# One decoder layer with 32 experts: big and small expert positions as two interleaved tracks of one-slot items, with a ninth weight slot

## The chip, the core and the metric

The kernel runs on one core of one Trainium2 chip. The metric is device time in microseconds (us) of one execution; the median of several runs is quoted with its lowest and highest. Engines: PE (TensorE, matmuls), DVE (VectorE), ACT (ScalarE), POOL (GpSimd) and SP (SyncE, which here issues DMAs).

## The reference

A residual stream of 512 tokens by 1024 channels passes one decoder layer in float32: RMSNorm, one input projection, a causal pooling mixer beside multi-head latent attention, an output projection and the residual; then the mixture of experts, which is what the change is about, and a final RMSNorm. Each token goes to 4 of 32 experts:

```python
logits = (ht @ w_router + b_router).astype(jnp.float32)
top_vals, top_idx = lax.top_k(logits, TOP_K)          # TOP_K = 4 of N_EXPERTS = 32
gates = jax.nn.softmax(top_vals, axis=-1)
...
gu = xblk @ w_gate_up[e] + b_gate_up[e]               # 1024 x 2048
gate = jnp.minimum(gu[:, :D_EXPERT], SWIGLU_LIMIT)
up = jnp.clip(gu[:, D_EXPERT:], -SWIGLU_LIMIT, SWIGLU_LIMIT)
act = gate * jax.nn.sigmoid(SWIGLU_ALPHA * gate) * (up + 1)
return act @ w_down[e] + b_down[e]                    # 1024 x 1024
```

So each expert needs 8 MiB of gate-and-up weights and 4 MiB of down weights, and all 32 are read: 384 MiB, about 403 MB.

## The kernel before

**The start.** Up to about 220 us the kernel does the attention half, the router and the choice of experts. Weights of expert position 0 are loaded beside it. Positions 0 to 31 are experts sorted by how many tokens chose them; which expert stands at a position is known on the chip only (`eid`, read into SP's registers).

**Big and small.** `KINDS` names each position B or S: 13 big ones (0, 4, 6, 8 and so on to 26) for up to 128 tokens, 19 small ones for up to 64. A loop after the main one takes what overflows.

- A *big* position has each weight tile split into a high and a low fp32r part: ACT casts (`mhi`, L875), DVE or POOL subtracts (`mlo`, L876), a helper `split` on 128x1024 halves with four buffers for each part. PE then does three matmuls for each product (`mm3`, L95 to L97, for gate and up; L979 for down). DVE or POOL is chosen by a fixed rule: POOL has 9 of a position's 24 halves, five in gate-and-up, four in down.
- A *small* position multiplies plain fp32 weights out of the slot in which they landed, 64 tokens wide, two such matmuls side by side in the array (L919 gate and up, L1001 down).

**The stages of a position.** `gather` transposes its tokens' rows (fetched by an indirect DMA on POOL's queue) into `xgh`/`xgl` or `xgs`; `gate_up` makes the gate and up sums in PSUM banks; `act`/`swiglu` is the nonlinearity on DVE and ACT; `turn` transposes the result (`ath`/`atl`, `ats`); `down` is the second product; `combine` scatters it to the tokens with matmuls into an `m` bank, and DVE adds that to `y` (L1059).

**The order.** The list `steps` says in which order whole `gate_up` and `down` stages stand: from position 6 on `gu` of a big, `gu` of a small, `dn` of the big, `dn` of the small. Other work (`rest`, `turned`, `arriving`, `gathering`) is put between the stage's items by generators, one step for each item. Before a big `gate_up`, `split_ahead` splits its first three items while the small `down` before it runs; a `down` has nothing split ahead. A scheduler then places the instructions of each engine in the order in which its own model finds them ready, so an engine's final order is not the program's line by line. Each engine runs its final order strictly in turn.

**Slots and loads.** Weights land in a ring of eight 1 MiB slots (one k of gate-and-up, or two k of down). SP issues the loads in ring order, and each waits until its slot has been read. PSUM has six `gu` banks, which all gate, up and down sums share, and two `m` banks.

Of the kernel before, what the change touches and what calls it, by code (L numbers as in the profile page):

```python
# [11 lines left out]
F32 = mybir.dt.float32  # L12
# [11 lines left out]
P = 128  # L24
# [17 lines left out]
assert len(KINDS) == 32 and KINDS[0] == "B" and "BB" not in KINDS and KINDS.endswith("SS") and NBIG % 2 == 1  # L42
# [3 lines left out]
NPRE = 3  # L46
# [54 lines left out]
def block_kernel(ctx: ExitStack, tc: tile.TileContext, xT, x, pos, vecs, w_in, w_pool, w_qb, w_kvb, w_out,  # L101
# [640 lines left out]
    def bank(tag):  # L742
        return pools["pm"].tile([P, T], F32, tag=tag, bufs={"gu": 6, "m": 2}[tag], name=tag)


    nslot = [0]

    def slot():
        i = nslot[0] % (NRING + 4 + NRINGB)
        nslot[0] += 1  # L750
        return (ring if i < NRING else qk if i < NRING + 4 else ringb).tile([P, 2 * D], F32, tag="slot", name="slot")
# [3 lines left out]
    def load_gate_up(r, w):  # L755
        for k in range(KD):
            wslots[r, "gu", k] = slot()
            dma(wslots[r, "gu", k], w[k * P:(k + 1) * P, :])

    def load_down(r, w, halves=False):  # L760

        n = 4 if halves else 2
        for c in range(2 if halves else 1):
            for k in range(KD // n):
                v = slot().rearrange("p (a d) -> p a d", a=n)
                cs = slice(c * T, (c + 1) * T) if halves else slice(0, D)
                dma(v, w[n * k * P:n * (k + 1) * P, cs].rearrange("(a p) d -> p a d", p=P))
                for a in range(n):
                    wslots[r, "dn", n * k + a, c] = v[:, a, :]
# [3 lines left out]
    def load_expert(r, e):  # L773

        gu, wdown[r] = (w[e] if isinstance(e, int) else w[bass.ds(e, 1)].rearrange("a k d -> (a k) d")
                        for w in (w_gate_up, w_down))
        load_gate_up(r, gu)

    load_expert(0, 0)
# [7 lines left out]
    def big(r):  # L787
        return r == "o" or KINDS[r] == "B"

# [18 lines left out]
    rows, idxs = {}, {}  # L808

    def fetch(r):  # L810
# [8 lines left out]
        rows[r] = hbp.tile([P, D], F32, tag="hb", name="xr")  # L819
# [39 lines left out]
    def slot_info(r, ax=None):  # L859
# [6 lines left out]
        sl = mo.tile([P, 7], F32, tag="sl", bufs=6, name="sl")  # L866
# [12 lines left out]
    presplit = {}  # L879

    def split_ahead(r):

        for k in range(NPRE):
            for hf in range(2):
                presplit[r, k, hf] = split(wslots[r, "gu", k][:, hf * D:(hf + 1) * D], G if hf else V)

    def gate_up(r, *beside):
        banks = [bank("gu") for _ in range(4 if big(r) else 2)]

        def biases():  # L890
            for c in range(4):
                bs = bias[:, c * T:(c + 1) * T]
                if big(r):
                    PE.matmul(banks[c], lhsT=m4b[0:96, r:r + 1].to_broadcast([96, P]), rhs=bs, start=r > 0, stop=r == 0)
                else:
                    q = 64 * (c % 2)
                    PE.matmul(banks[c // 2][q:q + 64, :], lhsT=m4b[0:96, r:r + 1].to_broadcast([96, 64]), rhs=bs,
                              start=True, stop=False)


        first = r == 0 or r == "o"
        if not first:
            biases()
        for k in range(KD):
            w = wslots.pop((r, "gu", k))
            if big(r):

                todo = [(hf, c) for hf in range(2) for c in range(2)] if k < KD - 1 else [
                    (hf, c) for c in range(2) for hf in range(2)]
                parts = [presplit.pop((r, k, hf), None) or  # L910
                         split(w[:, hf * D:(hf + 1) * D], G if (2 * k + hf) % 4 == 1 else V) for hf in range(2)]
                for hf, c in todo:
                    cs = slice(c * T, (c + 1) * T)
                    mm3(nc, banks[2 * hf + c], xg[r][0][:, k, :], xg[r][1][:, k, :], parts[hf][0][:, cs],
                        parts[hf][1][:, cs], first and k == 0, r != 0 and k == KD - 1)
            else:
                for c in range(4):
                    q = 64 * (c % 2)
                    PE.matmul(banks[c // 2][q:q + 64, :], lhsT=xg[r][:, k, :], rhs=w[:, c * T:(c + 1) * T],  # L919
                              start=False, stop=(k == KD - 1))  # L920
            for v in beside:
                next(v, None)
        if r == 0:
            biases()
        return banks
# [16 lines left out]
    def act(r, banks):  # L942
        return [swiglu(banks[c], banks[2 + c]) for c in range(2)] if big(r) else [swiglu(*banks)]

    def turn(r, us_):
# [5 lines left out]
        else:  # L951
            at = mo.tile([P, 2, 4, 64], F32, tag="ats", bufs=1, name="ats")
# [15 lines left out]
    def down(r, *beside):  # L968
        if big(r):
            hi, lo = actT.pop(r)  # L970
            banks = [bank("gu") for _ in range(2)]
            for k in range(KD):
                for v in beside:
                    next(v, None)
                wh, wl = split(wslots[r, "dn", k, 0], G if k % 2 == 0 else V)

                for n, (a, b) in enumerate(((hi, wh), (hi, wl), (lo, wh))):
                    for c in range(2):
                        PE.matmul(banks[c], lhsT=a[:, k, :], rhs=b[:, c * T:(c + 1) * T], start=(k == 0 and n == 0),  # L979
                                  stop=(k == KD - 1 and n == 2))  # L980
# [3 lines left out]
            for c in range(2):  # L984
                S.activation(yh[:, c], banks[c], AF.Copy, scale=ga_)  # L985
                V.scalar_tensor_tensor(yl[:, c], banks[c], ga_, yh[:, c].bitcast(F32), op0=ALU.mult, op1=ALU.subtract)  # L986
# [4 lines left out]
        else:  # L991
            at = actT.pop(r)
            db = bank("gu")
            par = KINDS[:r].count("S") % 2
            for k in range(KD):
                for v in beside:
                    next(v, None)
                w = wslots[r, "dn", k, 0]
                for q in range(2):
                    c = q ^ par  # L1000
                    PE.matmul(db[64 * q:64 * q + 64, :], lhsT=at[:, k, :], rhs=w[:, c * T:(c + 1) * T],  # L1001
                              start=(k == 0), stop=(k == KD - 1))
            if par == 0:
# [13 lines left out]
    def down_last(r, gf):  # L1017
# [7 lines left out]
        for c in range(2):  # L1025
            cs = slice(c * T, (c + 1) * T)

            pb = [bank("gu") for _ in range(NT)]
# [3 lines left out]
            db = bank("gu")  # L1032
            for k in range(KD):

                q = 64 * (k % 2)
                PE.matmul(db[q:q + 64, :], lhsT=at[:, k, :], rhs=wslots[r, "dn", k, c], start=(k < 2),  # L1036
                          stop=(k >= KD - 2))
# [9 lines left out]
    def combine(keys, with_bias=False, after=None):  # L1047


        parts = [(c, sc, [v[:, c] for v in yb[key]]) for key in keys for c, sc in enumerate(scat.pop(key))]  # L1050
# [233 lines left out]
    for r in range(6, E, 2):  # L1284
        steps += [("gu", r), ("gu", r + 1), ("dn", r), ("dn", r + 1)]
# [193 lines left out]
```

## Time and profile before

| | |
|---|---|
| median of 3 runs | 1412.95 us (1412.23 to 1414.8) |
| the profiled execution | 1414.44 us, of which the span from first to last instruction is 1412.7 us |
| PE busy in the span | 1271.1 us (90%), 5657 matmuls |
| DVE, ACT, POOL busy | 923.4 us (65%), 568.6 us (40%), 447.2 us (32%) |
| read from HBM | 430.24 MB, 308 GB/s over the span |

A busy PE is not a PE at its peak: matmuls overlap in the trace, so two that are 0.39 us long start 0.23 us apart. What a stretch is worth is read from how many matmuls it holds, from PE's idle time and from the granted clock (1.00 is 2.4 GHz, 0.50 is 1.2 GHz).

### The profile page before, as it was taken

To read this page: it belongs to the slowest core of one execution; us is meant where nothing else is said; L and a number is where in the kernel's file an instruction comes from. 1 tells how busy PE (TensorE), PEld (TensorE's weight loads), DVE (VectorE), ACT (ScalarE), POOL (GpSimd) and SP (SyncE) were. 2 spreads that over 40 slices of the span, in tenths; PEclk is the share of its full clock that TensorE was granted. 3 is DMA by queue.
4 is the path that set the end of the run, shared out by engine and by line. 5 is a ranking of instruction groups with operands and counts; after the bars stand their busy time and mean duration, and the time that the engine had idled before them with its cause. 6 is when DMAs were issued, how large, how long until landed. Compare 5 with 4: busy or idle time off the path is not lost.

```text
span 1412.7 us, 16684 instructions
## 1 busy us (share of the span) xinstructions
PE 1271.1 (90%) x5657; PEld 735.4 (52%) x5657; DVE 923.4 (65%) x1482; ACT 568.6 (40%) x819; POOL 447.2 (32%) x298
## 2 busy tenths in 40 slices
PE   7989977998989898998989898998899899999984
PEld 6756665534546464645546464645455454643322
DVE  6897689345757587676667586677766676853313
ACT  5477545113334353533334443534343535420112
POOL 1545363102143343323143443333241524330001
PEclk9999989899999999999999999999999999999997
DMA  7213336699999988897979899999979899899992
GB/s 296 75 58 118 138 131 224 241 413 424 411 399 351 336 333 337 328 347 291 346 302 353 330 354 338 340 336 348 359 293 365 328 329 360 340 333 382 424 421 107
DMA packets 87060, 435.71 MB, mean 308 GB/s; under 512 B 9209, under 2 KB 9337, under 8 KB 54202
## 3 DMA queue, kind: packets, MB, share of 16 engines
q1 hardware_dynamic: 82964, 420.57, 78.4%
q0 software_dynamic: 3808, 13.63, 2.5%
q8 instruction: 46, 0.75, 0.2%
q10 hardware_dynamic: 198, 0.39, 0.1%
q14 instruction: 44, 0.36, 0.1%
HBM read 430.24 MB, written 4.33 MB: 308 GB/s over the span
## 4 chain that ended last, share of the span: by engine, by line
PE 35%; issue 14%; DVE 5%; DMA 5%; POOL 4%; ACT 1%; POOLq 0%; DVEq 0%; ACTq 0%
PE gu L919 7%; PE gu L979 5%; PE gu L1001 5%; DMA slot<-in_w_down_dram 4%; PE gu L96 4%; PE gu L97 4%; PE gu L95 4%; POOL mlo L876 4%; DVE mlo L876 3%; PE m L1058 3%; DMA slot<-in_w_gate_up_dram 1%; ACT mhi L875 1%; PE m L849 1%; POOL xr L820 1%; PE gu L1036 1%
## 5 line engine op out<-in xcount | busy, mean ns | idle before, releaser
L876 POOL TENSOR_TENSOR mlo<-slot,mhi 128x1024 fp32r<-128x1024 f32 x116 | 316.8, 2737 | 586.8 <-ACT mhi L875 584.9
L876 DVE TENSOR_TENSOR mlo<-slot,mhi 128x1024 fp32r<-128x1024 f32 x196 | 350.8, 1817 | 40.9 <-ACT mhi L875 39.8
L875 ACT CAST mhi<-slot 128x1024 fp32r<-128x1024 f32 x312 | 317.6, 1049 | 148.8 <-PE gu L97 95.1
L919 PE MATMUL gu<-slot,xgs 128*64 128x512 f32 x1216 | 284.2, 600 | 2.2 <-DMA slot<-in_w_gate_up_dram 2.2
L96 PE MATMUL gu<-mlo,xgh 128*128 128x512 f32 x416 | 168.6, 405 | 19.7 <-DVE mlo L876 10.9
L97 PE MATMUL gu<-mhi,xgl 128*128 128x512 f32 x416 | 164.5, 395 | 0.0
L919 PEld LDWEIGHTS gu<-slot,xgs 128*64 128x64 f32 x1216 | 79.3, 136 | 154.9 <-issue 147.2
L1001 PE MATMUL gu<-slot,ats 128*64 128x512 f32 x576 | 139.9, 617 | 2.8 <-DMA slot<-in_w_down_dram 2.1
L1059 DVE TENSOR_TENSOR y<-y,m 128x512 f32<-128x512 f32 x120 | 81.0, 683 | 78.4 <-PE m L1058 77.2
L95 PE MATMUL gu<-mhi,xgh 128*128 128x512 f32 x416 | 125.2, 399 | 0.0
L936 ACT ACTIVATE as<-ag 128x512 f32<-128x512 f32 x45 | 28.4, 631 | 235.0 <-DVE ag L935 235.0
L96 PEld LDWEIGHTS gu<-mlo,xgh 128*128 128x128 f32 x416 | 79.2, 190 | 52.4 <-DVE mlo L876 16.9
L979 PE MATMUL gu<-mlo,ath 128*128 128x512 f32 x208 | 78.7, 463 | 24.4 <-POOL mlo L876 16.4
L979 PE MATMUL gu<-mhi,ath 128*128 128x512 f32 x208 | 73.3, 436 | 21.1 <-ACT mhi L875 20.4
L95 PEld LDWEIGHTS gu<-mhi,xgh 128*128 128x128 f32 x416 | 77.6, 190 | 20.4 <-issue 4.1
L97 PEld LDWEIGHTS gu<-mhi,xgl 128*128 128x128 f32 x416 | 79.4, 191 | 15.8
L820 POOL DMA_INDIRECT xr<-hrow,idx x22 | 33.8, 1536 | 143.7 <-DVE idx L818 80.5
L1001 PEld LDWEIGHTS gu<-slot,ats 128*64 128x64 f32 x576 | 37.4, 139 | 75.6 <-issue 67.0
L979 PE MATMUL gu<-mhi,atl 128*128 128x512 f32 x208 | 72.5, 433 | 0.0
L935 DVE TENSOR_SCALAR ag<-gu 128x512 f32<-128x512 f32 x45 | 31.0, 689 | 63.3 <-PE gu L919 60.5
L1014 DVE SCALAR_TENSOR_TENSOR ysl<-gu,sl,ysh 64x512 fp32r<-64x512 f32 x36 | 26.9, 748 | 67.1 <-ACT ysh L1012 66.6
L986 DVE SCALAR_TENSOR_TENSOR ybl<-gu,sl,ybh 128x512 fp32r<-128x512 f32 x26 | 18.3, 746 | 78.4 <-ACT ybh L985 78.4
(390 smaller groups left out, 1744.5 us busy)
## 6 DMA issues: line engine op xcount, KB each, us to landing
slot<-in_w_gate_up_dram SPq DMA_DIRECT2D x256, 1024.0 KB, 6.9
slot<-in_w_down_dram SPq DMA_DIRECT2D x128, 1024.0 KB, 7.5
wraw<-in_w_in_dram SPq DMA_DIRECT2D x16, 256.0 KB, 5.0
wraw<-in_w_out_dram SPq DMA_DIRECT2D x16, 256.0 KB, 2.5
xtraw<-in_xT_dram SPq DMA_DIRECT2D x8, 256.0 KB, 6.2
y<-in_x_dram SPq DMA_DIRECT2D x4, 512.0 KB, 6.8
hrow<-part POOLq DMA_DIRECT2D x8, 256.0 KB, 2.9
out_dram<-o SPq DMA_DIRECT2D x4, 512.0 KB, 3.6
```

The lines of the kernel that those rows point to most:

```text
L95: nc.tensor.matmul(out, lhsT=shi, rhs=mhi, start=first, stop=False)
L96: nc.tensor.matmul(out, lhsT=shi, rhs=mlo, start=False, stop=False)
L97: nc.tensor.matmul(out, lhsT=slo, rhs=mhi, start=False, stop=last)
L820: G.indirect_dma_start(out=rows[r], out_offset=None, in_=hrow, in_offset=bass.IndirectOffsetOnAxis(ap=idx[:, 0:1], axis=0), bounds_check=T ...
L875: S.copy(hi, src)
L876: eng.tensor_tensor(lo, src, hi.bitcast(F32), op=ALU.subtract)
L919: PE.matmul(banks[c // 2][q:q + 64, :], lhsT=xg[r][:, k, :], rhs=w[:, c * T:(c + 1) * T], start=False, stop=(k == KD - 1))
L935: V.tensor_scalar(g, gb, 7.0, None, op0=ALU.min)
L979: PE.matmul(banks[c], lhsT=a[:, k, :], rhs=b[:, c * T:(c + 1) * T], start=(k == 0 and n == 0), stop=(k == KD - 1 and n == 2))
L1001: PE.matmul(db[64 * q:64 * q + 64, :], lhsT=at[:, k, :], rhs=w[:, c * T:(c + 1) * T], start=(k == 0), stop=(k == KD - 1))
L1058: PE.matmul(pb, lhsT=a, rhs=b, start=(i == 0), stop=(i == len(todo) - 1))
L1059: V.tensor_tensor(y[:, t, cs], y[:, t, cs], pb, op=ALU.add)
```

## The change

Whole stages no longer stand one behind the other. Each position is cut into twelve *items* of one slot each, eight of `gate_up` and four of `down`. Two tracks are made: `tx` with the items of all big positions (and of the last small one), `ty` with the items of the other 18 small positions. A small search (`interleave`) merges them into one static `plan`: it pays for each change of track (`TURN`), for a `down` that starts fewer than `GAPX` = 5 small or `GAPY` = 2 big items after its own `gate_up` (`SHORT`), and for running ahead or behind of an even mix. The plan that results has 127 blocks, 64 of the big track and 63 of the small track, mostly two to five items long. Other edits go with it:

- Splits are made item by item (`split_item`), the next two items of the big track ahead of the one that PE multiplies, `down` items too. POOL has one half in four, DVE three; so of a position's 24 halves POOL has 6 and DVE 18.
- The six shared PSUM banks become four for the big track (`x`) and two for the small track (`y`).
- Loads are listed in the order in which slots are read: a small block's loads stand behind those of the big block after it, since that one is split ahead.
- A ninth slot is taken from one of the two `hb` buffers; fetched rows share the other.
- Down weights of the last position are loaded in four pieces as plan items.

```diff
+GAPX, GAPY, GAPEND = 5, 2, 3
+TURN, SHORT = 0.2, 3.0
...
-        return pools["pm"].tile([P, T], F32, tag=tag, bufs={"gu": 6, "m": 2}[tag], name=tag)
+        return pools["pm"].tile([P, T], F32, tag=tag, bufs={"x": 4, "y": 2, "m": 2}[tag], name=tag)
...
+    nring = NRING + 4 + NRINGB + 1
+    pair = []
...
+        if i == nring - 1:
+            if not pair:
+
+                pair.append(hbp.tile([P, 2, D], F32, tag="hb", name="xr"))
+            return hbp.tile([P, 2 * D], F32, tag="hb", name="slot")
...
-        rows[r] = hbp.tile([P, D], F32, tag="hb", name="xr")
+        rows[r] = pair[0][:, nfetch[0] % 2, :]
...
+    def split_item(r, what, k):
+
+        w = wslots.pop((r, what, k))
+        out_ = []
+        for hf in range(2):
+            out_.append(split(w[:, hf * D:(hf + 1) * D], G if nsplit[0] % 4 == 1 else V))
+            nsplit[0] += 1
+        presplit[r, what, k] = out_
...
-    steps = [("gu", 0), ("dn", 0), ("gu", 1), ("gu", 2), ("dn", 1), ("gu", 3), ("dn", 2), ("gu", 4), ("dn", 3),
-             ("gu", 5), ("dn", 4), ("dn", 5)]
-    for r in range(6, E, 2):
-        steps += [("gu", r), ("gu", r + 1), ("dn", r), ("dn", r + 1)]
...
+    tx = [v for r in range(E) if big(r) or r == E - 1 for v in items(r)]
+    ty = [v for r in range(E) if not big(r) and r < E - 1 for v in items(r)]
...
+                    c = cost + TURN * (t[4] != was) + SHORT * short + 0.04 * off * off
...
+    loads, late = [], []
+    for b in blocks:
+        if big(b[0][1]):
+            loads += b + late
+            late = []
+        else:
+            late += b
+    loads += late
...
+    for i, (what, r, k) in enumerate(plan):
...
+        for _ in gate_up(r, k) if what == "gu" else down(r, k):
+            step()
+        if big(r) and nsp < len(xorder) and nsp <= n + 2:
+            while nsp < len(xorder) and nsp <= n + 2:
+                split_item(xorder[nsp][1], xorder[nsp][0], xorder[nsp][2])
+                nsp += 1
```

Two places show what the scheduler makes of it. The first is ACT, where a big position's `down` begins. Before, on ACT: the casts `mhi` of the position's gate-and-up end, then come its two sigmoids (`as`), its two casts of the turned result (`ath`), eight pieces of the next big position's tokens (`xgh`), the small position's sigmoid, and only then the first casts of the `down` weights.

```order
L875 CAST mhi<-slot 128x1024 x14
L936 ACTIVATE as<-ag 128x512 x2
L962 CAST ath<-m 128x512 x2
L833 ACTIVATE xgh<-m,gs 128x128 x8
L936 ACTIVATE as<-ag 128x512
L875 CAST mhi<-slot 128x1024 x2
L966 COPY ats<-m 128x512
L875 CAST mhi<-slot 128x1024 x6
```

Now, at position 12, on ACT (L894 is now the cast, L958 the sigmoid, L985 `ath`, L852 `xgh`, L989 and L1042 copies of small positions): the two `mhi` casts behind the single sigmoid are already those of the first `down` item, the two behind `ats` those of the second.

```order
L1042 ACTIVATE ysh<-y,sl 64x512 x2
L894 CAST mhi<-slot 128x1024 x10
L958 ACTIVATE as<-ag 128x512
L894 CAST mhi<-slot 128x1024 x2
L989 COPY ats<-m 128x512
L894 CAST mhi<-slot 128x1024 x2
L958 ACTIVATE as<-ag 128x512 x2
L985 CAST ath<-m 128x512 x2
L852 ACTIVATE xgh<-m,gs 128x128
```

What moved: the first `down` casts went from behind `ath` and the next tokens to ahead of both. Of the twelve big positions after position 0 this is so for nine; for the other three they stand directly behind an `ath`.

The second place is PE, where a small `down` ends. Before (L1001 is the small `down`, L894 and L897 put biases into banks for the next big and small position, L1058 is `combine`, L95 to L97 the next big gate-and-up): the next small gate-and-up is a whole big stage away.

```order
L1001 MATMUL gu<-slot,ats 64x512 x8
L1058 MATMUL m<-ybh,sc 128x512 x2
L894 LDWEIGHTS m4b
L894 MATMUL gu<-bias,m4b 128x512
L1058 MATMUL m<-ybl,sc 128x512
L897 LDWEIGHTS m4b
L897 MATMUL gu<-bias,m4b 64x512
L897 LDWEIGHTS m4b
L897 MATMUL gu<-bias,m4b 64x512
L1058 MATMUL m<-ybl,sc 128x512
L1001 MATMUL gu<-slot,ats 64x512 x4
L95 MATMUL gu<-mhi,xgh 128x512 x4
```

Now (L1028 is the small `down`, L944 the small gate-and-up, L99 and L100 a big gate-and-up, L1091 `combine`): the next small gate-and-up follows a few matmuls behind it, its gate half first.

```order
L1028 MATMUL y<-slot,ats 64x512 x4
L1091 MATMUL m<-ybh,sc 128x512
L1091 MATMUL m<-ybl,sc 128x512
L99 MATMUL x<-mlo,xgh 128x512
L100 MATMUL x<-mhi,xgl 128x512
L99 MATMUL x<-mlo,xgh 128x512
L100 MATMUL x<-mhi,xgl 128x512
L1091 MATMUL m<-ybh,sc 128x512
L1091 MATMUL m<-ybl,sc 128x512
L944 MATMUL y<-slot,xgs 64x512 x2
L1091 MATMUL m<-ysh,ss_3081 128x512
L944 MATMUL y<-slot,xgs 64x512 x2
```

What moved: in 14 of the 17 handovers from one small position to the next the plan puts the new gate-and-up right behind the old `down`, where the up half needs the bank that this `down` has just filled. Over the whole expert part, runs of small matmuls that PE begins after another kind rise from 145 to 187 (the loop after the main one counted once in both).

## Rows read from the trace of the kernel before

**Rows 1.** Windows: us, busy of PE, PEld, DVE, ACT, POOL (count), clock, DMA share, GB/s.

```profile
222.00:380.00 158.00, 144.56 (x649) 75.30 (x648) 91.10 (x167) 46.67 (x60) 32.23 (x15) 0.95 0.91 359
380.00:1270.00 890.00, 814.27 (x3513) 471.35 (x3513) 615.80 (x792) 376.15 (x476) 311.55 (x120) 0.97 0.90 339
1270.00:1380.00 110.00, 101.80 (x452) 34.80 (x452) 33.05 (x54) 11.29 (x18) 1.12 (x1) 0.99 1.01 409
569.00:604.00 35.00, 35.00 (x152) 23.58 (x149) 22.63 (x19) 18.73 (x20) 14.10 (x5) 1.00 0.91 351
300.00:320.00 20.00, 19.83 (x101) 7.18 (x98) 7.03 (x18) 3.07 (x5) 0.99 (x1) 1.00 1.02 427
628.00:648.50 20.50, 16.50 (x54) 10.51 (x54) 15.98 (x16) 8.58 (x10) 12.36 (x5) 0.75 0.77 285
```

**Rows 2.** Groups by line, PE, 380 to 1270: busy, mean ns | idle before, releasers.

```profile
L919 PE MATMUL gu<-slot,xgs 128*64 128x512 f32 x768 | 180.7, 602 | 0.0
L96 PE MATMUL gu<-mlo,xgh 128*128 128x512 f32 x352 | 141.4, 402 | 16.1 <-DVE mlo L876 9.7 <-POOL mlo L876 6.4
...
L979 PE MATMUL gu<-mlo,ath 128*128 128x512 f32 x192 | 72.7, 462 | 24.4 <-POOL mlo L876 16.4 <-DVE mlo L876 8.0
L979 PE MATMUL gu<-mhi,ath 128*128 128x512 f32 x192 | 66.9, 432 | 20.4 <-ACT mhi L875 20.4
...
L849 PE MATMUL m<-ident,xr 128*128 128x128 f32 x136 | 22.8, 301 | 9.1 <-DVE sl L867 7.0 <-ACT ats L966 2.0
L959 PE MATMUL m<-ident,au 128*128 128x128 f32 x136 | 22.4, 287 | 2.5 <-DVE au L939 1.8 <-DVE y L1059 0.8
...
L865 PE MATMUL m<-aux,oh 128*128 128x4 f16 x96 | 5.9, 167 | 2.7 <-ACT ats L966 2.7
```

**Rows 3.** Timeline of PE at a big down: start, us, line, [idle <-releaser].

```profile
628.75 0.74 PE L979 MATMUL gu<-mhi,ath 128*128 128x512 f32 x2 [1.85 <-ACT mhi L875]
...
632.51 1.05 PE L979 MATMUL gu<-mhi,atl 128*128 128x512 f32 x2
633.37 1.05 PE L979 MATMUL gu<-mhi,ath 128*128 128x512 f32 x2
...
638.08 0.63 PE L979 MATMUL gu<-mhi,ath 128*128 128x512 f32 x2
638.54 0.63 PE L979 MATMUL gu<-mlo,ath 128*128 128x512 f32 x2
```

**Rows 4.** Timeline of ACT at the same place.

```profile
626.87 0.63 ACT L936 ACTIVATE as<-ag 128x512 f32<-128x512 f32 x1 [0.65 <-DVE ag L935]
...
627.66 1.98 ACT L875 CAST mhi<-slot 128x1024 fp32r<-128x1024 f32 x2
```

**Rows 5.** Timeline of PE where big and small matmuls alternate.

```profile
604.33 0.39 PE L97 MATMUL gu<-mhi,xgl 128*128 128x512 f32 x1
604.65 1.94 PE L919 MATMUL gu<-slot,xgs 128*64 128x512 f32 x8
...
607.66 3.65 PE L919 MATMUL gu<-slot,xgs 128*64 128x512 f32 x16
611.24 0.66 PE L959 MATMUL m<-ident,au 128*128 128x128 f32 x4
```

**Rows 6.** Timeline of ACT and DVE: a small down's bank is read out.

```profile
580.21 1.39 ACT L1012 ACTIVATE ysh<-gu,sl 64x512 fp32r<-64x512 f32 x2 [4.45 <-PE gu L1001]
...
581.64 1.53 DVE L1014 SCALAR_TENSOR_TENSOR ysl<-gu,sl,ysh 64x512 fp32r<-64x512 f32 x2 [5.56 <-ACT ysh L1012]
```

**Rows 7.** Instructions that read a slot: ns min/median/max, first and last start.

```profile
L876 DVE TENSOR_TENSOR mlo<-slot,mhi x196: 1203/1224/6451, 155.7 to 1258.9; 128x1024 fp32r<-128x1024 f32 x196
...
L876 POOL TENSOR_TENSOR mlo<-slot,mhi x116: 2366/2603/3401, 156.4 to 1257.6; 128x1024 fp32r<-128x1024 f32 x116
```

**Rows 8.** Waits of SP's queue: total us, times, longest.

```profile
SPq L758 <- DVE mlo L876: 327.9, 132, 12.9
```

**Rows 9.** DMA issues: KB each, median us from issue to landing.

```profile
slot<-in_w_gate_up_dram SPq DMA_DIRECT2D x256, 1024.0 KB, 6.9
```

More of the change, by code (lines that the diff above doesn't have):

```diff
@@ L877, in split @@
         return hi, lo
[L879 to L890, printed above, removed]
-            for c in range(4):
[L892 to L925, printed above, removed]
@@ new lines, in block_kernel, with biases @@
+    presplit, banks = {}, {}
+    nsplit = [0]
+    def split_item(r, what, k):
[5 more added lines that the diff above has]
+        presplit[r, what, k] = out_
+    def biases(r, first=True):
+        for c in range(4):
+            bs = bias[:, c * T:(c + 1) * T]
+            if big(r):
+                PE.matmul(banks[r][c], lhsT=m4b[0:96, r:r + 1].to_broadcast([96, P]), rhs=bs, start=first,
+                          stop=not first)
+            else:
+                q = 64 * (c % 2)
+                PE.matmul(banks[r][c // 2][q:q + 64, :], lhsT=m4b[0:96, r:r + 1].to_broadcast([96, 64]), rhs=bs,
+                          start=True, stop=False)
@@ L1026, in down_last @@
             cs = slice(c * T, (c + 1) * T)
-            pb = [bank("gu") for _ in range(NT)]
+            db = bank("y")
+            for k in range(KD):
+                q = 64 * (k % 2)
+                PE.matmul(db[q:q + 64, :], lhsT=at[:, k, :], rhs=wslots[r, "last", k, c], start=(k < 2),
+                          stop=(k >= KD - 2))
+            pb = [bank("x") for _ in range(NT)]
             for t in range(NT):
@@ L1288, in later @@
+    loads += late
+    xorder = [v for v in plan if big(v[1])]
     def later(g, n):
@@ new lines, in firsts, with step @@
+    def firsts(g):
+        return plan.index(("gu", g, 0))
+    fetch_at, turn_at = {}, {}
+    bigs = [r for r in range(E) if big(r)]
+    for g in groups:
+        if g == 1:
+            continue
+        turn_at[g] = firsts(g) - 7
+        if big(g):
+            turn_at[g] = max(turn_at[g], plan.index(("gu", bigs[bigs.index(g) - 1], KD - 1)) + 2)
+        fetch_at[g] = max(KD, turn_at[g] - 12)
+    queues = {"turn": [], "gather": [], "arrive": [], "rest": []}
+    def step(drain=()):
+        for name, q in queues.items():
+            while q:
+                if next(q[0], 0) == 0:
+                    q.pop(0)
+                    continue
+                if name not in drain:
+                    break
@@ L1386, in block_kernel @@
-        if waiting:
-            w, q = steps[i + 1]
-            if not big(q) and (w == "gu" or "s" in waiting and KINDS[:q].count("S") % 2 == 0):
-                rest, waiting = combine(waiting, 0 in waiting), []
-    assert not waiting
+            queues["turn"].append(later(turn(r, act(r)), 2))
+        if what == "dn" and k == KD // 2 - 1:
+            if big(r):
+                queues["rest"].append(combine([r], r == 0))
+            elif KINDS[:r + 1].count("S") % 2 == 0 and r != ty[-1][1]:
+                queues["rest"].append(combine(["s"]))
@@ L1414, in block_kernel @@
             pass
-        b4 = gate_up("o")
+        for k in range(KD):
+            split_item("o", "gu", k)
+            for _ in gate_up("o", k):
+                pass
+        b4 = banks.pop("o")
         us_ = [swiglu(b4[c], b4[2 + c], bl[:, c * T:(c + 1) * T], bl[:, D + c * T:D + (c + 1) * T]) for c in range(2)]
@@ L1418, in block_kernel @@
             pass
-        down("o")
+        for j in range(KD // 2):
+            split_item("o", "dn", j)
+            for _ in down("o", j):
+                pass
         gf = mo.tile([P, D], F32, tag="xgh", bufs=1, name="gf")
```

287 lines of the change are left out of this document (174 added, 113 removed).

## Prediction

> **What bounds the kernel now.** I read the windows first. Between 222 and 380, 380 and 1270, and 1270 and 1380 us, which together are the expert part, PE is busy 144.6 of 158, 814.3 of 890 and 101.8 of 110 us [rows 1]. The reader is to see that PE is the engine nearest to full in all three, and that it is not full: 13.4 + 75.7 + 8.2 = 97.3 us idle. The DMA share is 0.90 in the long middle stretch at 339 GB/s, while the same queue moves 427 GB/s where it is pressed (300 to 320 us). So memory is not the wall in the middle; it is in the last stretch, where only small positions are left (1.01, 409 GB/s).
>
> The groups by line then say what PE waits for in the middle [rows 2]. The idle time before matmuls is 16.1 + 24.4 + 20.4 + 9.1 + 2.5 + 2.7 = 75.2 of the 75.7 us. Of it 60.9 us are waits for a split (`mhi` from ACT, `mlo` from DVE or POOL), 14.3 us stand before transposes and slot lookups. Small gate-and-up matmuls, which read the slots directly, wait 0.0: loads come in time. So this is not a kernel short of an engine, but one in which splits are made too late.
>
> The timeline shows the dearest case, the first item of a big `down`: PE waits 1.85 us for ACT's cast [rows 3], which ACT begins only at 627.66, behind a small position's sigmoid [rows 4]. Behind this wait the granted clock drops: the stretch from 628 to 648.5 has 0.75 [rows 1], and two matmuls are 0.86 us apart from the next pair at 1.2 GHz (632.51 to 633.37) where they take 0.46 at 2.4 GHz (638.08 to 638.54) [rows 3]. The clock of 0.97 over 890 us means about 53 us at half speed; if PE is idle in about half of that (an estimate), the rest costs some 13 us more than at full clock. Another 4 us go so in the first stretch (0.95 over 158, 16 us at half speed, half of it idle).
>
> All that can be won in the expert part is therefore 97 + 17 = 114 us of 1158. A cross-check: where nothing waits, 152 matmuls take 35.0 us, 0.230 us each [rows 1]; 3513 of them would take 809 of the 890 us in the middle, so 81 us are lost there by this mixed pace, against 75.7 + 13 by the other account.
>
> **The change part by part.** PE's matmuls are the same in number and shape; what changes is their order, and who splits.
>
> *First item of a big `down`.* 20.4 us in 380 to 1270 [rows 2], where 192 matmuls of a form that a `down` has sixteen times make twelve `down` stages: 1.7 us each. The casts now stand ahead of `ath` at nine of twelve places, directly behind an `ath` at three. Nine waits go whole, three by half: 10.5/12 of 20.4, 17.9 us. What hides the casts is five small items between a big `gate_up` and its `down`: 40 matmuls at 0.23, 9 us, against 2 us for the two casts.
>
> *The other split waits.* 16.1 + 24.4 = 40.5 us. POOL's share falls from 116 of 312 halves to 78; a POOL half takes 2.60 us in the median, a DVE half 1.22 [rows 7]; and each big item is split two items, 24 matmuls or 5.5 us of PE, ahead. Bounds: nothing gained (worse is a rival below) and 40.5. I take 30, since the waits in the timeline are below 2 us [rows 3] and the lead exceeds them, but not all, since DVE runs in order and gets 38 more halves (46 us at 1.22, on an engine that is busy 616 of 890).
>
> *Transposes and lookups.* 14.3 us. The generators that feed them are started by plan position now. Bounds: 14 us gone or 14 more; I take 7 gone.
>
> *Clock.* 13 us in the middle. It fell where PE had stood idle; with (17.9 + 30 + 7)/75.7 = 73% of the idle time gone I take 9.5.
>
> *Both ends.* In the first stretch 13.4 idle and 4 of clock: small items now follow position 0's gate-and-up at once, but the start waits for the router as before; I take 6. In the last stretch two positions instead of five are left at the memory's pace; I take 4 of 8.2.
>
> Gains: 17.9 + 30 + 7 + 9.5 + 10 = 74.4 us.
>
> *Added: change of kind on PE.* 42 more runs of small matmuls (187 against 145). From the last big matmul to the first small one 0.32 us pass (604.33 to 604.65) instead of 0.23, and eight small ones take 1.86 alone but 1.79 in a run of sixteen (3.58 from 607.66 to 611.24) [rows 5]: about 0.16 a run, 6.9 us.
>
> *Added: bank waits.* With two `y` banks the up half of a small `gate_up` waits until the `down` before it is read out: ACT from 580.21 for 1.39, DVE from 581.64 for 1.53, 2.96 us in all [rows 6]. This stands at 14 handovers: at most 41 us, at least 0. Between the two the scheduler put four big matmuls, `combine` and the gate halves of two items, some 2.6 us; I take 0.4 each, 6 us. What is queued behind such a wait on PE is the next big item. With four `x` banks a big `gate_up` likewise needs the banks of the `down` before it; in the plan seven of twelve follow directly. The reads are as long, PE has the gate half (six matmuls, 1.4 us) to fill; 0 to 21 us, I take 4.
>
> *The ninth slot and the load order* have no price of their own: small matmuls waited for no load before [rows 2]. SP waits in turn for each slot, 327.9 us in 132 waits for DVE's splits alone [rows 8], so loads are held back by slots and not by the memory. Rows share a buffer now; POOL's fetch can wait there, and its splits behind it. I take nothing.
>
> Sum: 74.4 - 6.9 - 6 - 4 = 57.5 us less. Span 1412.7 - 57.5 = 1355.2; the profiled execution took 1.7 more than its span, so 1356.9; the median of the runs is 1.5 below it: 1355 us.
>
> The weights must then come at 403 MB (158 x 359 + 890 x 339 + 110 x 409, in us by GB/s) in 1158 - 57 = 1101 us, 366 GB/s, against 427 in the 20 us and 409 in the 110 us where the queue is pressed [rows 1].
>
> **Rivals.**
>
> *All comes back.* With the splits always ahead, 114 - 6.9 = 107 us: 1306. For it: gate-and-up stretches such as 569 to 604 lose nothing today [rows 1]. Against it: banks, and an order fixed beforehand.
>
> *DVE and POOL set the pace.* DVE's half takes 1.22 us, at worst 6.45 [rows 7], longer than a POOL half and its own: it stands while POOL subtracts. If the two take turns, two big items need 3 x 1.22 + 2.60 = 6.3 us against 24 x 0.23 = 5.5 on PE, and the lead of two items melts in runs of big items. Then the 30 us of late splits stay, and half of the clock's: 57.5 - 30 - 5 = 22, 1390. Against it: between big items stand small ones that need no split.
>
> *Small blocks wait for their loads (slower).* A small block's loads are queued behind all of the next big block, whose third and later items keep their slots until the small block has run, in a ring in strict turn. A load takes 6.9 us from issue to landing [rows 9]. If each of the 63 small blocks finds its first slot not landed by t, 63 t is lost: from t = 0.91 us (57.5/63) on the change is slower, and at 2 us the time is 1481. For it: the 12.9 us for which SP once stood [rows 8]. Against it: nine slots against an average need of 86% of 427 GB/s.
>
> *The memory cannot hold the rate.* Under a load that is even and long it may give no more than the 359 GB/s of the first stretch [rows 1]: 403/0.359 = 1123 us for the expert part, 1378 at the end. Against it: the 409 GB/s of the last stretch, held for 110 us. The Trainium skill has this as a rule (DMA: Bandwidth & Descriptors, Specifications): the limit of HBM for one core is about 358 GB/s; an estimate by that figure is 403/0.358 = 1126 us and 1381 at the end. The trace goes past that figure in the first stretch by a hair, in the last one and in the 20 us by far.
>
> *It does not do what it says.* The scheduler reorders by its own model; big items still stand in runs of three or more in places. Gains and added costs cancel: about 1412, either sign.
>
> **How the numbers follow.** Forecast 0.48, all back 0.13, DVE and POOL 0.17, late loads 0.13, memory 0.04, no effect 0.05. The range from 1302 to 1402 holds the forecast, nearly all of the second and third case and the memory's, about 0.8; outside are late loads, no effect, and the tails. Under 0.2% (3 us) a measurement of this kernel cannot tell a change. Faster: 0.48 + 0.13 + 0.15 + 0.04 + 0.02 = 0.82; within 0.2%: 0.01 + 0.02 = 0.03; slower: 0.13 + 0.01 + 0.01 = 0.15.
>
> **What would show it.** Right: PE's idle time before the first matmuls of a big `down` near 3 us instead of 20.4; all split waits near 10 instead of 60.9; the clock at 0.99 over the middle; DMA near 365 GB/s and even. The added costs: idle before small gate-and-up and before biases that names ACT or DVE reads of a `y` or `x` bank, about 10 us in all. DVE as pacemaker: split waits that name DVE stay at 30 us or more. Late loads: PE idle before small matmuls that names a DMA, over 20 us. Wrong altogether: a PE busy share of the expert part that is no higher than today's 92%.

## The result: slower, and the profile after

The changed kernel takes 1435.2 us (median of 4 runs, 1433.54 to 1436.28), the kernel before 1412.8: a ratio of 1.0155, 95% interval 1.0137 to 1.0173. The forecast was 1355 with a range of 1302 to 1402. The profiled execution has a span of 1434.6 us, 21.9 more than before, at a clock of 0.955 instead of 0.959.

The windows of the changed kernel, columns as in [rows 1]:

```profile
222.00:380.00 158.00, 144.21 (x640) 83.63 (x639) 108.96 (x191) 66.04 (x84) 34.67 (x17) 0.95 0.81 319
380.00:1270.00 890.00, 805.38 (x3445) 434.09 (x3445) 555.40 (x831) 333.24 (x432) 182.78 (x77) 0.96 0.88 341
1270.00:1380.00 110.00, 103.74 (x448) 49.79 (x446) 58.29 (x78) 27.78 (x34) 13.47 (x6) 1.00 0.93 361
1380.00:1435.00 55.00, 36.78 (x164) 14.80 (x160) 19.57 (x62) 12.89 (x28) 5.04 (x4) 0.89 0.56 225
```

In the middle stretch PE is busy 805.4 of 890 us against 814.3, with 68 matmuls fewer, and the DMA share has not risen. Over 222 to 1380 us PE's busy share is 91.0% (before: 91.6%), the mark that the prediction set for "wrong altogether". Loads did not hold up the small gate-and-up matmuls, which wait 0.0. The groups of PE in the middle, columns as in [rows 2], say what took the place of the splits:

```profile
L944 PE MATMUL y<-slot,xgs 128*64 128x512 f32 x876 | 211.5, 608 | 0.0
L99 PE MATMUL x<-mlo,xgh 128*128 128x512 f32 x316 | 130.3, 412 | 15.8 <-DVE mlo L895 12.6 <-DVE idx L832 1.8 <-POOL mlo L895 1.3
...
L1004 PE MATMUL x<-mhi,ath 128*128 128x512 f32 x160 | 58.5, 438 | 10.8 <-ACT mhi L894 8.0 <-ACT ath L985 2.9
L1004 PE MATMUL x<-mlo,ath 128*128 128x512 f32 x160 | 55.4, 428 | 3.5 <-POOL mlo L895 2.7 <-DVE mlo L895 0.5
...
L1091 PE MATMUL m<-ysh,ss 128*128 128x512 f32 x56 | 26.4, 480 | 8.9 <-DVE y L1092 4.7 <-ACT ysh L1042 4.2
...
L982 PE MATMUL m<-ident,au 128*128 128x128 f32 x132 | 24.4, 315 | 41.8 <-DVE au L961 40.6 <-DVE y L1092 1.0
```

L99, L1004 and L982 answer to L96, L979 and L959 of before. Split waits fell from 60.9 us to about 27 (15.8 + 10.8 + 3.5, less the 1.8 and 2.9 that are no splits, and 1.5 at L98). The wait for the nonlinearity, in front of the transposes of `turn`, rose from 2.5 to 41.8. What was won at one place was lost at the other. A third wait is new: `combine` (L1091) stood 8.9 us in front of its `ysh` matmuls, until ACT had read out a small `down` or DVE had added an `m` bank to `y`. In all, PE's idle time in the middle went from 75.7 to 84.6 us.

Idle time is only a part of the 21.9 us. This is the last window before:

```profile
1380.00:1413.00 33.00, 14.34 (x56) 6.54 (x52) 12.64 (x52) 9.17 (x22) 4.99 (x4) 0.76 0.21 82
```

With it and [rows 1], PE was idle 115.7 us from 222 us to the end; now it is 122.5, 7 us more. The other 15 are busy time, 1090.1 us instead of 1075.0. Some 6 of them are 27 more matmuls (at 0.23 us) that now stand behind 222 us. The rest is pace: 0.232 us for a matmul instead of 0.230, in which the clock and the changes of kind were not separated.

Its dearest case is 7.30 us. First PE, at the end of the gate-and-up of small position 11, where that of big position 12 has just ended too (timeline: start, us, line, idle before):

```profile
679.79 5.37 PE L944 MATMUL y<-slot,xgs 128*64 128x512 f32 x24
687.94 0.66 PE L982 MATMUL m<-ident,au 128*128 128x128 f32 x4 [2.78 <-DVE au L961]
695.90 1.11 PE L982 MATMUL m<-ident,au 128*128 128x128 f32 x4 [7.30 <-DVE au L961]
```

Then DVE in that time, and POOL:

```profile
687.19 0.69 DVE L961 TENSOR_TENSOR au<-au,as 128x512 f32<-128x512 f32 x1
687.80 3.37 DVE L895 TENSOR_TENSOR mlo<-slot,mhi 128x1024 fp32r<-128x1024 f32 x1
691.10 0.68 DVE L957 TENSOR_SCALAR ag<-x 128x512 f32<-128x512 f32 x1
...
692.89 2.35 DVE L895 TENSOR_TENSOR mlo<-slot,mhi 128x1024 fp32r<-128x1024 f32 x2
695.16 0.68 DVE L961 TENSOR_TENSOR au<-au,as 128x512 f32<-128x512 f32 x1
```

```profile
687.67 2.42 POOL L895 TENSOR_TENSOR mlo<-slot,mhi 128x1024 fp32r<-128x1024 f32 x1 [11.60 <-ACT mhi L894]
```

Both tracks are at their nonlinearity at once, and PE's order has no other matmul there. Three such places (424 to 432, 688 to 696 and 961 to 965 us) make 29.6 of the 41.8 us. DVE's final order puts three split halves of the coming `down` between its steps, and the first takes 3.37 us instead of 1.22, since POOL began a half 0.13 us earlier; DVE's ends 1.08 us behind POOL's.

How could both end together, when the plan keeps five small items between a big gate-and-up and its `down`? Counted in the traces, these are the gate-and-up and down matmuls that PE really has between the two (position 0 left out):

| | big: median, least | small: median, least |
|---|---|---|
| before | 56, 56 | 38, 32 |
| the plan asks for | 40 | 24 |
| the changed kernel | 16, 8 | 20, 0 |

At 0.23 us each, 56 are 13 us and 16 are 3.7. The plan was shorter than the old order, and the scheduler, which puts ready work first by its own model, shortened it again.

### The profile page after: what moved, and what is told of

It reads as the page before. It is cut to its first block, busy times and chain, and to the rows that moved or that the text cites. A ratio compares the mean times of both kernels' runs of the same rounds, so it can differ in the third digit from the quotient of the medians.

```text
span 1434.6 us, 16692 instructions
## 1 busy us (share of the span) xinstructions
PE 1282.2 (89%) x5657; PEld 726.7 (51%) x5657; DVE 906.8 (63%) x1568; ACT 561.7 (39%) x819; POOL 332.1 (23%) x260
## 5 line engine op out<-in xcount | busy, mean ns | idle before, releaser
L894 ACT CAST mhi<-slot 128x1024 fp32r<-128x1024 f32 x312 | 315.5, 1046 | 216.9 <-PE x L100 157.0
L895 POOL TENSOR_TENSOR mlo<-slot,mhi 128x1024 fp32r<-128x1024 f32 x78 | 203.8, 2613 | 743.1 <-ACT mhi L894 743.0
L895 DVE TENSOR_TENSOR mlo<-slot,mhi 128x1024 fp32r<-128x1024 f32 x234 | 326.2, 1410 | 38.1 <-ACT mhi L894 37.5
L944 PE MATMUL y<-slot,xgs 128*64 128x512 f32 x1152 | 280.5, 611 | 0.5 <-DVE xgs L874 0.5
L99 PE MATMUL x<-mlo,xgh 128*128 128x512 f32 x416 | 172.7, 415 | 17.4 <-DVE mlo L895 14.1
L100 PE MATMUL x<-mhi,xgl 128*128 128x512 f32 x416 | 165.4, 400 | 0.0
L944 PEld LDWEIGHTS y<-slot,xgs 128*64 128x64 f32 x1152 | 74.3, 138 | 134.5 <-issue 132.6
L98 PE MATMUL x<-mhi,xgh 128*128 128x512 f32 x416 | 138.1, 417 | 3.1 <-ACT mhi L894 3.1
L1028 PE MATMUL y<-slot,ats 128*64 128x512 f32 x576 | 139.8, 611 | 0.0
L958 ACT ACTIVATE as<-ag 128x512 f32<-128x512 f32 x45 | 28.4, 631 | 254.2 <-DVE ag L957 254.1
L99 PEld LDWEIGHTS x<-mlo,xgh 128*128 128x128 f32 x416 | 79.9, 192 | 65.1 <-DVE mlo L895 25.2
L98 PEld LDWEIGHTS x<-mhi,xgh 128*128 128x128 f32 x416 | 78.3, 194 | 28.0 <-ACT mhi L894 6.8
L100 PEld LDWEIGHTS x<-mhi,xgl 128*128 128x128 f32 x416 | 79.7, 192 | 17.8 <-issue 1.6
L1004 PE MATMUL x<-mhi,ath 128*128 128x512 f32 x208 | 74.7, 433 | 11.8 <-ACT mhi L894 8.3
L957 DVE TENSOR_SCALAR ag<-y 128x512 f32<-128x512 f32 x18 | 12.4, 690 | 105.2 <-PE y L944 105.2
L1004 PE MATMUL x<-mlo,ath 128*128 128x512 f32 x208 | 71.3, 424 | 4.7 <-POOL mlo L895 3.3
L982 PE MATMUL m<-ident,au 128*128 128x128 f32 x180 | 32.3, 306 | 46.6 <-DVE au L961 45.2
L1028 PEld LDWEIGHTS y<-slot,ats 128*64 128x64 f32 x576 | 37.1, 138 | 69.3 <-issue 68.5
L1004 PE MATMUL x<-mhi,atl 128*128 128x512 f32 x208 | 70.0, 415 | 0.5 <-DVE atl L986 0.5
L1004 PEld LDWEIGHTS x<-mhi,ath 128*128 128x128 f32 x208 | 38.8, 198 | 41.1 <-issue 18.3
```

The source lines that it names most:

```text
L98: nc.tensor.matmul(out, lhsT=shi, rhs=mhi, start=first, stop=False)
L99: nc.tensor.matmul(out, lhsT=shi, rhs=mlo, start=False, stop=False)
L100: nc.tensor.matmul(out, lhsT=slo, rhs=mhi, start=False, stop=last)
L894: S.copy(hi, src)
L895: eng.tensor_tensor(lo, src, hi.bitcast(F32), op=ALU.subtract)
L944: PE.matmul(banks[r][c // 2][q:q + 64, :], lhsT=xg[r][:, k, :], rhs=w[:, c * T:(c + 1) * T], start=False, stop=(k == KD - 1))
```

## The experiments

They ran in four rounds (e1 to e4, e5 to e8, e9 to e12, e13 and e14), each on a chip of its own. Ratios are to the kernel before on the same chip, which took 1414.1 to 1416.2 us there and 1412.8 beside the changed kernel; a difference in us between two rounds is good to some 3 us.

| run | us | ratio, 95% interval |
|---|---|---|
| e1 loads in plan order | 1415.6 | 1.0008, 0.9983 to 1.0032 |
| e2 order fixed | 1394.4 | 0.9860, 0.9814 to 0.9906 |
| e3 e1 and e2 | 1420.3 | 1.0033, 1.0005 to 1.0062 |
| e4 eight slots | 1415.7 | 1.0015, 0.9996 to 1.0035 |
| e5 ninth slot late | 1421.8 | 1.0043, 1.0023 to 1.0062 |
| e6 e2 and e5 | 1393.7 | 0.9842, 0.9801 to 0.9883 |
| e7 fixed, spaced, loads by due time | 1335.4 | 0.9438, 0.9401 to 0.9474 |
| e8 e2 without POOL | 1364.8 | 0.9648, 0.9600 to 0.9697 |
| e9 e7 without POOL | 1318.7 | 0.9340, 0.9308 to 0.9372 |
| e10 e7, order free | 1413.6 | 0.9996, 0.9979 to 1.0014 |
| e11 changed, without POOL | 1394.0 | 0.9862, 0.9832 to 0.9892 |
| e12 before, without POOL | 1357.6 | 0.9611, 0.9574 to 0.9648 |
| e13 e6, loads by due time | 1351.3 | 0.9539, 0.9505 to 0.9573 |
| e14 e7 with eight slots | 1330.7 | 0.9406, 0.9377 to 0.9435 |

### Is it the order that the scheduler made?

e1 changes the list of loads alone:

```diff
-    loads, late = [], []
...
+    loads = list(plan)
```

> The loads are listed in the order of the plan, no small block behind the next big one; nothing else is changed. In the changed kernel PE waits 46.6 us before the transposes of the nonlinearity's result, because its final order begins a big down 2.2 to 11.6 us of PE work after its own gate-and-up (median 6, by item times of 0.23 us a matmul), where the plan has five small items or more, 9.3 us. Theory A (the scheduler unmade the plan, since in its model the small items' loads land late): with plain load order the leads in the final order are 8.1 to 9.9 us, the idle time before those transposes falls below 20 us, and the time to 1400 +- 10. Theory B (the loads in reading order do help, splits get their weights sooner): slower than 1435, SP waits longer for splits, PE waits for mhi and mlo rise above 34 us. Theory C (DVE has too many splits, whatever the order): idle before transposes stays above 35 us, 1430 +- 5.

The list moved PE's order as theory A said: 32 matmuls (median and least) instead of 16 before a big `down`. The waits of PE, 380 to 1270 us (us in total, times, longest):

```profile
PE x L1004 <- ACT mhi L894: 14.7, 11, 1.9
PE m L982 <- DVE au L961: 10.5, 13, 2.4
PE x L99 <- DVE mlo L895: 10.5, 8, 1.8
PE x L99 <- POOL mlo L895: 10.1, 5, 3.7
```

The wait for the nonlinearity is a quarter of what it was, but split waits are back, as theory B said: 52.6 us instead of 27 (that big items' weights come later is likely, but was not measured). The time, 1415.6, is neither theory's.

e2 leaves the loads and ties each matmul of the plan behind the one before it, without a wait:

```diff
+    def in_turn(i):
+        if prev[0] is not None:
+            tc.add_manual_dep(i.ins, prev[0].ins.name, mybir.DependencyInfo(
+                mybir.DependencyClass.NoSync, mybir.DependencyReason.DATA), reason="plan")
+        prev[0] = i
```

> Loads as in the changed kernel; the order of the gate-and-up and down matmuls on PE is fixed to that of the plan by ordering edges without waits, so that the scheduler can move other work only. Theory A: the loads were late in the model alone, so PE does not wait for a DMA in front of small matmuls (under 5 us in all), leads are 10 to 12 us for big downs, idle before transposes under 20 us, 1395 +- 15. Theory B (the scheduler was right, small items' weights do land late): PE waits for DMAs in front of small matmuls by over 20 us, the time is 1435 or more. Theory C: idle before transposes stays above 35 us, 1430 +- 10.

Now 40 and 24 matmuls stand there, 41 us are gone, and split waits in the same window are 0.5 us. The waits that are left there:

```profile
PE m L991 <- DVE au L970: 25.9, 12, 4.1
PE y L927 <- DVE ysl L1055: 14.7, 8, 4.1
...
PE y L953 <- DMA slot<-in_w_gate_up_dram: 5.1, 6, 2.0
```

Weights of small items come late by 5.1 us in all, so the scheduler had moved them for little. Two waits of the plan's own remain: the nonlinearity, and the `y` banks (L927, a bias), which the free order had hidden.

e3 has both edits.

> Both: loads in the order of the plan and the plan's order fixed on PE. Theory A: as good as either alone, 1395 +- 15, since each of the two restores the plan. If the order of loads matters by itself on the chip, it differs from the run with the fixed order alone by more than 5 us, to either side. Theory C: 1430.

26 us slower than e2: the order of loads counts by itself. It is no faster than e1 either, so with this list of loads the tie gains nothing. Its waits for splits:

```profile
PE x L99 <- DVE mlo L897: 23.3, 22, 2.8
PE x L1013 <- ACT mhi L896: 13.5, 9, 1.9
PE x L1013 <- DVE mlo L897: 10.3, 7, 3.6
```

### What does the ninth slot cost?

e4 is the changed kernel with `nring = NRING + 4 + NRINGB`.

> The changed kernel with eight weight slots, as before; all else is unchanged. Theory A gives the ninth slot no price of its own: 1435 +- 4. Rival (the ring is what holds the new order together, loads are held back by slots): 1450 or more, with PE waits for DMA or for splits that rise by 10 us.

Both theories failed: eight slots are faster, by 19.5 us. In the changed kernel the first load into the ninth slot waits for a buffer of the attention half (waits of SP's queue):

```profile
SPq L774 <- DVE hb L609: 33.0, 1, 33.0
```

e5 lets that slot join in the second pass:

```diff
-        i = nslot[0] % nring
+        n = nslot[0]
+        i = n if n < nring - 1 else (n - nring + 1) % nring
```

> The changed kernel, but the ninth slot joins the ring only in its second pass; the first pass has eight slots as before. In the changed kernel the load into the ninth slot stands 33 us in SP's queue for a buffer of the attention half, with every load behind it; with eight slots the first small item began 8 us earlier (249.9 instead of 257.9 us) and the run was 20 us faster in all. Theory A: the whole of the 20 us follows from that one wait and from what it shifts; then this run is at 1416 +- 5. Theory B: 8 us are the wait, the other 12 are the ring of nine itself; then 1427 +- 4. Theory C (neither: the order that the scheduler's model makes of it decides): outside both.

13.4 of the 19.5 us come back, between the two theories. The intervals of e4 and e5 meet, so it is not shown that e4 is better. The first small matmuls start at 257.95 us in the changed kernel and at 249.63 in e5:

```profile
257.95 4.54 PE L944 MATMUL y<-slot,xgs 128*64 128x512 f32 x10 [0.47 <-DVE xgs L874]
```

```profile
249.63 5.22 PE L944 MATMUL y<-slot,xgs 128*64 128x512 f32 x12 [1.51 <-DVE xgs L874]
```

So the start is 8.3 us earlier. Behind the load that waited stand the last two gate-and-up loads of position 0 (SP's queue in the changed kernel, then in e5):

```profile
202.30 0.93 SPq L768 DMA_DIRECT2D slot<-in_w_gate_up_dram  x2
```

```profile
185.83 0.82 SPq L768 DMA_DIRECT2D slot<-in_w_gate_up_dram  x2
```

The gain is not this wait alone. The scheduler's final order on PE is another one in each of the three kernels, and PE's wait for the nonlinearity in 380 to 1270 us is 31.2 us in e4 and 26.4 in e5 instead of 40.6. With the order fixed (e6: e2 and e5) the same edit gives nothing:

> The run with the plan's order fixed on PE (1394 us), with the ninth slot joining in the second pass. The first small item should begin at about 247 instead of 254.6 us. If the gains add: 1387 +- 3. If the fixed order takes the 8 us back at the next wait for a load or a bank: 1394 +- 3.

The first big item after position 0 begins 7 us earlier than in e2 and the end is the same. And in the spaced kernel below, eight slots (e14) are as good as nine: the intervals meet, so a gain from the ninth slot was not found anywhere.

> The spaced run (1335.4 us) with eight slots. Theory A (loads are ahead of their readers by more than a slot): 1335 +- 4. Theory B (with nothing else waiting, the ring is next): PE waits for splits or loads rise by 10 us, 1348 or more. Theory C (as in the free order, fewer slots are faster): under 1328.

### Are the plan's distances too short?

e7 is e6 with a wider plan, and with loads in the order in which each item is read or split:

```diff
-GAPX, GAPY, GAPEND = 5, 2, 3
+GAPX, GAPY, GAPZ, GAPEND = 5, 4, 2, 3
...
+                    short = max(0, (GAPY if ty[y_][0] == "dn" else GAPZ) - gy) if ty[y_][2] == 0 else 0
...
+    due = {v: at_[xs_[max(0, n - 2)]] + 0.5 for n, v in enumerate(xs_)}
+    loads = sorted(plan, key=lambda v: due.get(v, at_[v]))
```

> The same, and the plan is spaced: a small down comes at least four big items after its gate-and-up instead of two, and the next small gate-and-up at least two big items after that down instead of none; loads stand in the order in which each item is read or split (big ones two items ahead of PE), which the wider spacing needs. With the plan's order fixed and unspaced, PE still waited 28.3 us for the nonlinearity (DVE au) and 19.9 us for DVE to read out a y bank. Theory A (both are distances in the plan that were set too short): together under 12 us, clock 0.975 or more, 1387 - 40 = 1347 +- 12. Theory B (DVE is short of time there, whatever the distance): they stay above 30 us, 1380 or more. Theory C (loads are late when the plan is spaced): PE waits for DMAs or splits by over 25 us.

The time is theory A's, and the middle window shows a PE that is nearly full at 0.99 of the clock:

```profile
380.00:1270.00 890.00, 849.94 (x3803) 474.50 (x3803) 595.68 (x896) 367.56 (x460) 175.25 (x82) 0.99 0.95 376
```

But the mechanism is so only in part. The waits for `y` banks are gone, and 48 matmuls (11 us) stand between a small gate-and-up and its `down`; yet 25.4 us for the nonlinearity stay. They stand behind the ends of big gate-and-ups:

```profile
562.35 0.39 PE L100 MATMUL x<-mhi,xgl 128*128 128x512 f32 x1
565.43 0.66 PE L991 MATMUL m<-ident,au 128*128 128x128 f32 x4 [2.69 <-DVE au L970]
566.02 3.53 PE L953 MATMUL y<-slot,xgs 128*64 128x512 f32 x8
```

PE reaches the transposes (L991), which the scheduler still places, before DVE is done, while 40 small matmuls, the first eight of which then run without a wait, are still to come before this position's `down`. A run with the transposes tied as well was not made.

e13 has the loads of e7 without its spacing:

> The plan of the change with its order fixed on PE and the ninth slot joining late (1393.7 us), but with the loads in the order in which each item is read or split (big ones two items ahead) as in the spaced run; no spacing. Theory A (spacing gave the 58 us): 1394 +- 6, waits for the nonlinearity and for the y banks remain at 40 us or more. Theory B (the order of the loads gave it): 1345 +- 10. Half and half: 1365.

1351.3: of the 58 us from e6 to e7, 42 are the load order and 16, on top of it, the spacing (whose plan also has fewer blocks, 107 instead of 127); spacing with the old list was not run. From e6 to e13 PE's idle time in 380 to 1270 us falls from 67.7 to 51.0 and the clock rises from 0.97 to 0.99; how the 42 us divide was not measured. Waits of SP's queue, e6 and then e13:

```profile
SPq L770 <- DVE mlo L897: 450.2, 87, 22.2
```

```profile
SPq L770 <- DVE mlo L897: 244.1, 78, 10.4
```

The change put a small block's loads behind a whole big block of two to five items, while only two are split ahead; so SP stood up to 22.2 us in front of a big item's slot, with the small items' loads behind it. "Reading order" was meant and was not what the list had.

e10 is e7 without the ties on PE:

> The spaced plan with its load order and the late ninth slot, but PE's order left to the scheduler. Its final order begins seven of the twelve big downs after position 0 only 4.0 to 4.6 us of PE work behind their gate-and-up, where the plan has 7.5 to 9.4. Theory A (a plan helps only if the final order keeps it): waits for the nonlinearity and for ath above 25 us, 1365 to 1400. Theory B (spacing is what counts, the scheduler's moves are harmless): 1335 +- 5.

1413.6, slower than theory A's range: the 78 us from e10 to e7 hang on the ties alone. Big downs again have 16 matmuls in front of them, and the waits are those of the changed kernel (380 to 1270):

```profile
PE m L982 <- DVE au L961: 31.2, 15, 4.1
PE x L98 <- ACT mhi L894: 9.9, 9, 1.5
```

### Does POOL's share pay?

In e8 (from e2), e9 (from e7), e11 (from the changed kernel) and e12 (from the kernel before) the one edit is to give POOL no half (in e12 at the three places where the kernel before chooses it):

```diff
-            out_.append(split(w[:, hf * D:(hf + 1) * D], G if nsplit[0] % 4 == 1 else V))
+            out_.append(split(w[:, hf * D:(hf + 1) * D], V))
```

> The run with the plan's order fixed on PE (1394 us), with all 312 split halves on DVE and none on POOL. In that run DVE's splits took longer than the 1.22 us of one alone wherever POOL held the memory port. Theory A (POOL's share costs more in held-up DVE work than it saves): DVE's busy time rises by less than 78 x 1.22 = 95 us, waits for the nonlinearity fall below 20 us, 1385 +- 8. Theory B (DVE needs the relief): waits for splits and for the nonlinearity rise by 15 us or more, 1410 +- 10. If neither: 1394 +- 4.

> The spaced run (1335.4 us) with all splits on DVE. Without POOL's share the run with the fixed but unspaced order fell by 29.6 us, because DVE's own operations no longer stood for POOL (its 78 more splits cost DVE 60 us, not 95). In the spaced run 28.7 us of waits for the nonlinearity are left and hardly any waits for splits. Theory A (held-up DVE work is what is left): those waits fall below 16 us, the time to 1318 +- 8. Theory B (spacing has already taken the gain, DVE off the path): 1335 +- 4. Theory C (DVE becomes short, 379 us of splits in less time): waits for splits above 10 us, slower than 1340.

> The changed kernel (1435 us) with all splits on DVE and nothing else undone. Theory A (the coincidence of nonlinearity and splits on DVE, stretched by POOL's hold on the port, is a good part of the loss): waits before the transposes fall from 46.6 to 30 us or less, 1410 +- 10. Theory B (only the order counts): 1435 +- 5. Theory C (DVE needs the relief when the order is as it is): slower than 1440.

> The kernel before, with all splits on DVE; nothing of the change is in it. It says whether POOL's share was already a loss there. 116 POOL halves move to DVE, whose 196 halves took 350.8 us, 1.82 each. Theory A (DVE stood for POOL): 312 halves at 1.22 take 381 us, 30 more than now, waits for POOL (22.8 us) go, and the time falls by 15 to 40 us, to 1372 to 1398. Theory B (DVE is then the engine that is late): waits for splits by DVE rise by more than the 22.8 us that go, 1412 or more.

All four gain: 29.6, 16.8, 41.2 and 57.1 us, three of them more than any theory gave. In e8 and e9 PE's order is tied, so a new order of PE's does not explain it there. Split halves in the changed kernel, and in e12 (columns as in [rows 7]):

```profile
L895 DVE TENSOR_TENSOR mlo<-slot,mhi x234: 1202/1218/4031, 155.7 to 1339.8; 128x1024 fp32r<-128x1024 f32 x117
```

```profile
L876 DVE TENSOR_TENSOR mlo<-slot,mhi x312: 1202/1218/1228, 155.0 to 1204.2; 128x1024 fp32r<-128x1024 f32 x156
```

In e12 every half takes 1.20 to 1.23 us; in the changed kernel some take up to 4.03, and up to 6.45 in the kernel before [rows 7]. The Trainium skill (SBUF — State Buffer, Who interferes with whom) calls the port pair that the two engines share an exclusive lock, and says that a DVE instruction with two SBUF inputs contends with a GpSimd instruction that reads SBUF. The trace agrees: POOL's 2.42 us from 687.67 on end at 690.09, and DVE's half, begun at 687.80, ends 1.08 us later, about the time that one takes alone. What PE still waits for in e12 (380 to 1270):

```profile
PE gu L979 <- ACT mhi L875: 19.1, 12, 1.6
PE gu L96 <- DVE mlo L876: 7.8, 9, 1.4
PE m L959 <- DVE au L939: 5.6, 12, 0.6
PE gu L979 <- DVE mlo L876: 4.5, 11, 0.5
```

The 22.8 us of waits for POOL [rows 2] are gone, and DVE's fell too, from 17.7 to 12.3. The 57 us are more than these waits; the middle window's clock rose from 0.97 to 0.99, and how the rest divides was not measured. In e9 the waits for the nonlinearity hardly fell (25.6 us in 380 to 1270), so theory A's time there was right for a reason that it did not name.

e9 beats both kernels: 1318.7 us, a ratio of 0.9340.

## Why the prediction was wrong, step by step

Two steps failed. The sum took the plan for PE's final order (40 and 24 matmuls before a `down`), which had 16 and 20; with the order tied (e2) 41 us come back. And it gave the load order "no price"; in the tied order the list as it was meant is worth 42 us (e6 to e13). With both, and the ninth slot late, e13 takes 1351.3 us, next to the forecast of 1355. That does not confirm the sum: in the middle e13 has no split waits, where the sum leaves 13 us, and 23.6 us for the nonlinearity, where it leaves 7 for all transposes and lookups.

- *What bounds the kernel*: half right. Splits were late, but the cheapest cause stood in the rows and was not priced: 22.8 us of waits for POOL and DVE halves of up to 6.45 us. Both were read as a matter of who does how many halves.
- *First item of a big `down`*: 17.9 us expected, 12.4 got (20.4 to 8.0; over all thirteen stages 20.4 to 8.3). The step that failed is its cover, "five small items between a big `gate_up` and its `down`: 40 matmuls at 0.23, 9 us". That is the plan. PE's final order had 16, 3.7 us. The order of ACT was counted, that of PE was not. With PE's order tied (e2) none of these waits is left in the middle.
- *Other split waits*: 30 expected, about 22 got.
- *Transposes and lookups*: this is the term that turned the sign. "I take 7 gone" of 14.3, with 14 more as the bound; the rows after give 42 us, 28 more. The lookups and the tokens' transposes did gain (11.8 to 0.2 us); the whole loss is the nonlinearity. It was priced by the generators that feed it and not by what PE has to do between a gate-and-up and its `down`, where the transposes stand: the change cut that from 56 and 38 matmuls to 16 and 20, and let both tracks end together. The bound was wrong for the same reason.
- *Clock*: 9.5 us expected back; the clock fell from 0.97 to 0.96 instead, as idle time moved and did not go.
- *Both ends*: 10 expected, about 2 got (8.2 to 6.3 us idle in 1270 to 1380). The first stretch is as before (144.2 busy): PE waits there once, 6.4 us, for the rows of the first small position (L868, DMA `xr`), which the sum does not have. The ninth slot, for which it takes "nothing", cost 13.4 us by e5 in the free order and none in the fixed one (e6).
- *Bank waits*: 10 expected. Waits for an `x` or `y` bank were 1.0 in the middle, but the 8.9 us of `combine`, in part for the read-out of a small `down`, are not in the sum; where the order was kept (e2) the `y` banks cost 14.7, more than the 6 taken.
- *Change of kind*: 6.9 us, not tested by itself.
- *Rivals*: late loads were named with the right place (SP in front of a big item's slot) but did not decide the result: small gate-and-up waits 0.0 for them; in a kept order their list is worth 42 us. DVE and POOL taking turns was right as a mechanism (41 us by e11), but it was in the kernel before as well (57 us). "All comes back", 1306, is near what e9 reaches, by other edits. The memory rival is refuted by e9, whose middle window moves 382 GB/s:

```profile
380.00:1270.00 890.00, 858.40 (x3858) 476.60 (x3854) 627.60 (x960) 367.00 (x460) 19.67 (x18) 0.99 0.96 382
```

## What to carry to other kernels

Where a scheduler stands between a plan and the chip, measure the plan's distances in the final order of the engine that is to be covered, in microseconds of its work, and compare them with the old order's; if a plan is worth having, tie it and list the loads in the order in which it really reads them (e13, 84 us below the changed kernel). Where two streams are interleaved, look for the places at which their serial parts (here the nonlinearity) fall together. Before relieving an engine by a neighbour, take the neighbour's share away once: here that single edit won 57 us, where the whole change lost 22.

## What had not been expected of the hardware

A half given to POOL relieved DVE of far less than its 1.22 us. DVE was busy with halves for 326.2 us in the changed kernel (234 of them) and 372.2 in e11 (all 312), 0.59 us for each of the 78 that POOL had; in the kernel before and in e12 it was 350.8 and 366.0, 0.13 us for each of 116. And one load that waits for its buffer at the front of SP's queue, 33.0 us, went with a first small matmul 8.3 us later.
